# The attention gate's two rows: two f32r products each in place of one f32 product, with the row's two parts in places that rotary rows held at first

## The chip, the cores and the metric

One Trainium2 chip, one core. A time is the device time of one launch in microseconds (us), the median of several runs. Lines of the kernel are named L1088 and so on; engines are TensorE (PE; PEld is its weight load), VectorE (DVE), ScalarE (ACT), GpSimd (POOL) and SyncE (SP), which issues the DMAs.

## The reference

One decoder block on 1024 tokens of 1024 columns, all in float32. The part that matters here is the modulation: one vector `c` gives six rows of 1024 numbers, and the third, `gt_a`, is the gate that scales what the attention half adds to the stream.

```python
cond = jax.nn.silu(c)
mod = (cond @ w_ada[l] + b_ada[l]).astype(x.dtype)
sh_a, sc_a, gt_a, sh_m, sc_m, gt_m = [m[:, None, :] for m in jnp.split(mod, N_MOD, axis=-1)]
h = rms_norm(x, g_attn_pre[l]) * (1 + sc_a) + sh_a
proj = h @ w_in[l]
...
y = mixed @ w_out[l]
x = x + gt_a * rms_norm(y, g_attn_post[l])
h = rms_norm(x, g_mlp_pre[l]) * (1 + sc_m) + sh_m
y = jnp.square(jax.nn.relu(h @ w_up[l])) @ w_down[l]
x = x + gt_m * rms_norm(y, g_mlp_post[l])
```

Between `proj` and `mixed` stand rotary embedding, sliding-window attention with sinks (heads A) and a mixture of three dilated windows (heads B).

## The kernel before

**Number formats.** A product of two f32 tiles takes PE two passes. Where it matters the kernel splits an f32 tile in two parts of the shorter format f32r (a cast gives the high part, a subtraction of it from the original the low part) and multiplies the parts: three products high x high, high x low and low x high where both sides are split (the projection, L920, L921, L923), two where one side is exact in f32r. The subtraction for weights is L555, for probabilities L1326, and the casts are L550 and L1322.

**Stages.** Up to about 113 us the first tokens are normalised, turned round and projected. From there to about 560 us the projection of the rest (`pj`) and the attention run side by side; then come the output projection, and from about 640 us the MLP.

**The order of the work.** The program is written down by a planner in Python (`Sched`). Every step has an engine, a planned duration, the steps that it depends on, the places (`Res`: counted resources, one for each ring of buffers) that it takes and gives back, and a priority. The planner keeps a clock for each engine and always gives out the step that can start first by these clocks. PE's steps lie in streams (projection, scores, transposes, products with values, and so on), each in its own order; the planner picks among their heads. A step of VectorE or GpSimd may have both as its alternatives (the subtraction at L555 has), and the planner gives it to the one that would end first. So a planned duration that changes, or a place given back at another time, changes the order of all engines behind it, and on which of two engines a step runs. On the chip each engine runs its own instructions strictly in that order and waits on semaphores; SyncE's DMAs too are issued in order, and a DMA that has to wait for its buffer holds up those behind it.

**A slice of projection weights.** A load into `w_st` (L541, 128x512, two places), a cast on ScalarE into `w_hl` (L550), a subtraction on VectorE or GpSimd (L555) that frees the `w_st` place. Then the slice serves four groups of three products.

**A pair of attention.** Scores `s_ps` on PE (L1258 for A, L1203 for B), their maximum on VectorE, the exponential on ScalarE (L1278, with the running sum read out), transposes `pt_ps` on PE (L1315 or L1308 and L1311), the split of the transposed tile into `ph` (high part ScalarE L1322, low part VectorE L1326), and the products with the values `o_ps` (L1350, L1338, L1341, L1343), read out by a copy on ScalarE (L1385) and stored (L1395).

**The modulation rows, `ada_piece`.** Three of the rows, which the front does not need at once, are made in 24 pieces between the attention's items: six groups `g` of 512 columns with four pieces each; groups 0 and 1 are the attention gate `gt_a`, 2 to 5 the shift and scale of the MLP. (Groups 6 and 7, the gate of the MLP, go the same way later, during the MLP.) Each piece loads 512 KB of `w_ada` into `wa_st` (L1054) and adds its products with `cond` into `ada_acc` on GpSimd (L1065, L1069, L1070; there is one place for `ada_acc`, `r_adacc`). What is left is a sum over the 128 partitions. For gate rows a product with a tile of ones (step `fin`) sums them and leaves the row in every partition at once. For groups 6 and 7 the accumulator is cast on ScalarE (L1098) and subtracted on VectorE (L1101) into the parts `acc_hl`, and two f32r products with `ones_h` follow (L1086); for groups 0 and 1 one f32 product takes `ada_acc` as it is (L1088), and gives `r_adacc` back. Then come two loads of 256 KB into `gate_st` (the bias, L1112, and the gain, L1113), an addition (L1118) and a multiplication (L1124) on VectorE, and a store to `gate_d` (L1128).

**The places.** `stage(...)` gives one of five places of 4 KB a partition (`r_stg`), shared by `wa_st`, `gate_st`, the split activations `hl` and others. The pool `early` has three more such places: two hold the rotary tables' rows (`turned` L722, `rows` L749) near the start, and all three serve the output projection's first tiles at the end of the attention.

Of the kernel before, what the change touches and what calls it, by code (L numbers as in the profile page):

```python
# [10 lines left out]
F32 = mybir.dt.float32  # L11
F32R = mybir.dt.float32r
# [7 lines left out]
P = 128  # L20
# [157 lines left out]
class Sched:  # L178
# [21 lines left out]
    def op(self, eng, dur, emit, deps=(), **kw):  # L200

        o = self.step(dur, emit, deps, **kw)
        o.alts = None
        if isinstance(eng, str):
            self.queue[eng].append(o)
        else:
            o.alts = dict(zip(eng, zip(dur, emit)))
            for e in eng:
                self.queue[e].append(o)
        return o.ev  # L210

    def pe_op(self, stream, dur, emit, deps=(), **kw):
        o = self.step(dur, emit, deps, **kw)
        o.alts = None
        self.pe.setdefault(stream, []).append(o)
        return o.ev
# [116 lines left out]
def t_as(n):  # L333
    return 0.2 + 0.00083 * n


def t_dv(n):
    return 0.066 + 0.00104 * n
# [19 lines left out]
def hybrid_block(ctx: ExitStack, tc: tile.TileContext, x, positions, w_ada, b_ada, g_attn_post, w_in, w_out,  # L358
# [3 lines left out]
    V, A, G, T = nc.vector, nc.scalar, nc.gpsimd, nc.tensor  # L362
# [3 lines left out]
    op, pe_op = sc.op, sc.pe_op  # L366

    def pool(name, bufs=1, side="left", space=None, stack=ctx):
        kw = dict(name=name, bufs=bufs, reuse_waits="tile")
        if space is not None:  # L370
            kw["space"] = space
        else:
            kw["side"] = side
        return stack.enter_context(tc.tile_pool(**kw))
# [9 lines left out]
    def ring_r(name):  # L384

        return ph2.right.tile([P, 1024], F32, name=name, tag="right")
# [7 lines left out]
    r_stg, r_w, r_wst, r_hl = Res(5), Res(WR), Res(WS), Res(0)  # L394
    r_u, r_raw, r_h2, r_wo = Res(0), Res(0), Res(0), Res(0)
# [11 lines left out]
    ones = const.tile([P, P], F32, name="ones")  # L407
# [21 lines left out]
    early = pool("early", 3)  # L429
# [25 lines left out]
    def stage(name):  # L455
        if st.stgp is None:
            return ring_r(name)
        return st.stgp.tile([P, 1024], F32, name=name, tag="stg")

    def load(emit, nbytes, deps=(), takes=(), prio=5, gives=(), after=None, n=1):  # L460
        return op("SP", nbytes / (345e3 if prio > -500 else 370e3), emit, deps, takes=takes, prio=prio, gives=gives, after=after, n=n)
# [30 lines left out]
    r_wa, r_acc = Res(NWA), Res(2)  # L492
# [90 lines left out]
    e = op("ACT", 0.1, lambda: A.activation(cond[:], c_raw, AF.Exp, scale=-1.0), [e_c], prio=0)  # L583
# [32 lines left out]
    e = op("DVE", 4.2, f_turns, [e_pos, e_c], prio=1)  # L616

    def f_sin():
# [5 lines left out]
                prio=1)  # L624
# [150 lines left out]
    def tables_b():  # L775
# [12 lines left out]
       prio=8)  # L788
# [254 lines left out]
    ada = Tok()  # L1043
    ada.i, ada.acc, ada.e, ada.raw, ada.gate = 0, None, Ev(0.0), {}, {}
    e_mod = {}
    r_adacc = Res(1)

    def ada_piece(i, eng, accp, psum, r_ps, r_acc=None):
        g, jp = divmod(i, 4)
        col = 2 * D + g * 512  # L1050

        def f_load():
            ada.raw[i] = stage("wa_st")
            nc.sync.dma_start(ada.raw[i][:].rearrange("p (j n) -> p j n", j=2),  # L1054
                              ada_view[:, 2 * jp:2 * jp + 2, col:col + 512])
        el = load(f_load, 524288, takes=[(r_stg, 1)], prio=20)

        def f_acc():
            wa = ada.raw.pop(i)[:].rearrange("p (j n) -> p j n", j=2)
            if jp == 0:  # L1060
                ada.acc = accp()
            for j in range(2):
                cj = cond[:, 2 * jp + j:2 * jp + j + 1]
                if jp == 0 and j == 0:
                    eng.tensor_scalar(ada.acc[:, :512], wa[:, 0], cj, 1.0, ALU.mult, ALU.mult)  # L1065
                elif eng is V:
                    V.scalar_tensor_tensor(ada.acc[:, :512], wa[:, j], cj, ada.acc[:, :512], ALU.mult, ALU.add)
                else:
                    G.tensor_scalar(wa[:, j], wa[:, j], cj, 1.0, ALU.mult, ALU.mult)  # L1069
                    G.tensor_tensor(ada.acc[:, :512], ada.acc[:, :512], wa[:, j], ALU.add)  # L1070
        e = op("DVE" if eng is V else "POOL", 1.2 if eng is V else 4.1, f_acc,
               [el, ada.e], takes=[(r_acc or r_adacc, 1)] if jp == 0 else [], gives=[(r_stg, 1)], prio=9)
        ada.e = e
        if jp < 3:
            return
        b = []
        row = g in (0, 1, 6, 7)
        n0 = (g % 2) * 512

        hl = []  # L1080

        def f_fin():
            b.append(psum())
            if row and g > 5:
                for i in range(2):
                    T.matmul(b[0][:, :512], ones_h[:], hl[0][:, i], start=(i == 0), stop=(i == 1))  # L1086
            elif row:
                T.matmul(b[0][:, :512], ones[:], ada.acc[:, :512], start=True, stop=True)  # L1088
            else:
                for k in range(4):  # L1090
                    T.matmul(b[0][:, k:k + 1], ada.acc[:, k * P:(k + 1) * P], ones[:, 0:1], start=True, stop=True)
        if row and g > 5:
            acc = []

            def f_ah():
                acc.append(ada.acc)
                hl.append(stage("acc_hl")[:].rearrange("p (s n) -> p s n", s=2).bitcast(F32R))
                A.copy(hl[0][:, 0], acc[0][:, :512])  # L1098

            def f_al(eng):  # L1100
                return lambda: eng.tensor_tensor(hl[0][:, 1], acc[0][:, :512], hl[0][:, 0].bitcast(F32), ALU.subtract)  # L1101
            e = op("ACT", t_as(512), f_ah, [e], takes=[(r_stg, 1)], prio=4)
            ada.e = e
            e = op("DVE", t_dv(512), f_al(V), [e], gives=[(r_acc or r_adacc, 1)], prio=4)
        ef = pe_op("fin", (0.46 if g > 5 else 0.86) if row else 0.45, f_fin, [e], takes=[(r_ps, 1)],
                   gives=[(r_stg if row and g > 5 else r_acc or r_adacc, 1)])
        if row:
            gate, gp = (gate_d[0], g_attn_post) if g < 2 else (gate_d[1], g_mlp_post)

            def f_gl():  # L1110
                ada.gate[g] = t = stage("gate_st")
                nc.sync.dma_start(t[:, 0:512], b_ada[0:1, col:col + 512].to_broadcast([P, 512]))  # L1112
                nc.sync.dma_start(t[:, 512:1024], gp[0:1, n0:n0 + 512].to_broadcast([P, 512]))  # L1113
            eg = load(f_gl, 524288, [e], takes=[(r_stg, 1)], prio=19)

            def f_g1():
                t = ada.gate[g]
                V.tensor_tensor(t[:, 0:512], b[0][:, :512], t[:, 0:512], ALU.add)  # L1118
            e1 = op("DVE", t_dv(512), f_g1, [ef, eg], gives=[(r_ps, 1)], prio=4)

            def f_g2():
                t = ada.gate[g]
                if g < 2:
                    V.tensor_tensor(t[:, 0:512], t[:, 0:512], t[:, 512:1024], ALU.mult)  # L1124
                else:
                    V.scalar_tensor_tensor(t[:, 0:512], t[:, 0:512], D ** 0.5, t[:, 512:1024], ALU.mult, ALU.mult)
            e2 = op("DVE", t_dv(512), f_g2, [e1], prio=4)
            e_mod[g] = load(lambda: nc.sync.dma_start(gate[:, n0:n0 + 512], ada.gate[g][:, 0:512]), 262144, [e2],  # L1128
                            gives=[(r_stg, 1)], prio=18)
        else:  # L1130
            k0 = n0 // P

            def f_c():
                if g < 4:
                    V.tensor_tensor(s_m[:, k0:k0 + 4], b[0][:, 0:4], cols[:, 40 + k0:44 + k0], ALU.add)
                else:
                    V.tensor_tensor(g_m[:, k0:k0 + 4], b[0][:, 0:4], b1m[:, k0:k0 + 4], ALU.add)
                    V.tensor_tensor(g_m[:, k0:k0 + 4], g_m[:, k0:k0 + 4], cols[:, 16 + k0:20 + k0], ALU.mult)
            e_mod[g] = op("DVE", 0.15, f_c, [ef], gives=[(r_ps, 1)], prio=4)

    def feed_ada():
        if st.d > 1.0 + ada.i * 4.1 / NADA and ada.i < NADA:
            ada_piece(ada.i, G, lambda: adp.tile([P, 512], F32, name="ada_acc", tag="ada_acc", bufs=1), lambda: px.tile([P, 512], F32, name="ada_ps", tag="x"), r_x)
            ada.i += 1
        return ada.i == NADA
# [1097 lines left out]
```

## Time and profile before

| what | us |
|---|---|
| median of 3 runs (lowest, highest) | 1121.01 (1121.01, 1121.78) |
| the profiled execution's own time | 1121.31 |
| its span, first to last instruction | 1119.5 |
| PE busy, 0 to 60 us | 56.00 of 60 |
| PE busy, 60 to 113 us | 51.20 of 53 |
| PE busy, 113 to 235 us | 120.28 of 122 |
| PE busy, 235 to 550 us | 313.65 of 315 |
| PE busy, 550 to 1080 us | 530.00 of 530 |
| PE busy, 1080 us to the end | 31.00 of 39.5 |

The table cuts the span into stretches and asks for the busy time of PE in each. Matmuls are pipelined, so a product that started just before a wait still counts as busy for a while. The granted TensorE clock was 0.998 of full speed over the whole execution. The two `fin` steps of groups 0 and 1 lie at 113.8 and 173.4 us; everything that the change touches is between them and some 60 us behind.

### The profile page before, as it was taken

To read this page: it belongs to the slowest core of one execution; us is meant where nothing else is said; L and a number is where in the kernel's file an instruction comes from. 1 tells how busy PE (TensorE), PEld (TensorE's weight loads), DVE (VectorE), ACT (ScalarE), POOL (GpSimd) and SP (SyncE) were. 2 spreads that over 40 slices of the span, in tenths; PEclk is the share of its full clock that TensorE was granted. 3 is DMA by queue.
4 is the path that set the end of the run, shared out by engine and by line. 5 is a ranking of instruction groups with operands and counts; after the bars stand their busy time and mean duration, and the time that the engine had idled before them with its cause. 6 is when DMAs were issued, how large, how long until landed. Compare 5 with 4: busy or idle time off the path is not lost.

```text
span 1119.5 us, 15561 instructions
## 1 busy us (share of the span) xinstructions
PE 1102.1 (98%) x5393; PEld 917.0 (82%) x5393; DVE 822.5 (73%) x1391; ACT 629.2 (56%) x1092; POOL 245.0 (22%) x313
## 2 busy tenths in 40 slices
PE   8999999999999999999999999999999999999996
PEld 7778787888888888888888888888888888888885
DVE  7868777666677676689798564798643996537998
ACT  8759776464665666576674335653154632247542
POOL 2158758657741231110000000000000000000003
PEclk9999999999999999999999999999999999999999
DMA  9766675554514643656761279521578113584104
GB/s 351 219 197 183 189 226 198 177 178 160 204 33 151 238 136 97 220 226 234 279 244 38 82 239 335 200 62 52 198 262 304 36 57 111 190 316 154 39 19 150
DMA packets 94110, 195.39 MB, mean 175 GB/s; under 512 B 9008, under 2 KB 31664, under 8 KB 94032
## 3 DMA queue, kind: packets, MB, share of 16 engines
q1 hardware_dynamic: 94032, 194.40, 50.4%
q8 instruction: 43, 0.70, 0.2%
q14 instruction: 35, 0.29, 0.1%
HBM read 141.80 MB, written 33.03 MB: 156 GB/s over the span
## 4 chain that ended last, share of the span: by engine, by line
PE 84%; DVE 9%; issue 2%; ACT 2%; DMA 2%; POOL 0%; SPq 0%; DVEq 0%; POOLq 0%; ACTq 0%
PE mlp_ps L2056 17%; PE mlp_ps L2055 17%; PE mlp_ps L2057 17%; PE pj L920 4%; PE pj L923 4%; PE pj L921 4%; PE s_ps L1203 3%; PE y_ps L1609 2%; PE y_ps L1611 2%; PE y_ps L1610 2%; PE o_ps L1338 2%; PE pt_ps L1308 1%; PE o_ps L1350 1%; PE pt_ps L1311 1%; DVE hw L1819 1%
## 5 line engine op out<-in xcount | busy, mean ns | idle before, releaser
L2055 PE MATMUL mlp_ps<-hw 128*128 128x512 f32 x896 | 348.9, 389 | 0.2 <-DVE u L2092 0.2
L2057 PE MATMUL mlp_ps<-hw 128*128 128x512 f32 x896 | 348.6, 389 | 0.0
L2056 PE MATMUL mlp_ps<-hw 128*128 128x512 f32 x896 | 348.6, 389 | 0.0
L2055 PEld LDWEIGHTS mlp_ps<-hw 128*128 128x128 f32 x896 | 168.2, 188 | 35.8 <-DVE u L2092 0.6
L2057 PEld LDWEIGHTS mlp_ps<-hw 128*128 128x128 f32 x896 | 168.2, 188 | 35.0
L2056 PEld LDWEIGHTS mlp_ps<-hw 128*128 128x128 f32 x896 | 168.2, 188 | 34.6
L1819 DVE TENSOR_TENSOR hw<-w,hw 128x1024 fp32r<-128x1024 f32 x96 | 114.5, 1219 | 96.3 <-ACT hw L1812 96.1
L1812 ACT CAST hw<-w 128x1024 fp32r<-128x1024 f32 x96 | 97.7, 1048 | 126.9 <-PE mlp_ps L2057 86.2
L2165 POOL TENSOR_TENSOR st<-st,nhalf 128x1 f32<-128x1 f32 x8 | 8.0, 1011 | 591.8 <-DVE st L2163 591.8
L920 PE MATMUL pj<-hw,w_hl 128*128 128x512 f32 x240 | 101.7, 424 | 0.0
L923 PE MATMUL pj<-hw,w_hl 128*128 128x512 f32 x240 | 94.7, 394 | 0.0
L921 PE MATMUL pj<-hw,w_hl 128*128 128x512 f32 x240 | 94.4, 393 | 0.0
L1326 DVE TENSOR_TENSOR ph<-pt_ps,ph 128x512 fp32r<-128x512 f32 (+1 forms) x110 | 68.8, 646 | 29.3 <-ACT ph L1322 29.0
L1812 ACT CAST hw<-u 128x1024 fp32r<-128x1024 f32 x48 | 48.6, 1051 | 63.2 <-PE mlp_ps L2057 63.2
L1322 ACT CAST ph<-pt_ps 128x512 fp32r<-128x512 f32 (+1 forms) x110 | 58.1, 555 | 28.2 <-PE pt_ps L1311 24.5
L1819 DVE TENSOR_TENSOR hw<-u,hw 128x1024 fp32r<-128x1024 f32 x48 | 56.9, 1217 | 17.8 <-ACT hw L1812 17.8
L1229 ACT ACTIVATE p_sb<-p_sb,mn 128x128 f32<-128x128 f32 (+3 forms) x64 | 49.7, 776 | 32.2 <-DVE mn L1222 31.7
L1234 POOL TENSOR_SCALAR p_sb<-p_sb,den 128x128 f32<-128x128 f32 (+3 forms) x64 | 49.4, 778 | 77.3 <-DVE den L1232 65.2
L2113 DVE TENSOR_TENSOR yacc<-yacc,mlp_ps 128x512 f32<-128x512 f32 x96 | 62.0, 680 | 3.3 <-PE mlp_ps L2057 3.3
L1070 POOL TENSOR_TENSOR ada_acc<-ada_acc,wa_st 128x512 f32<-128x512 f32 x42 | 55.0, 1310 | 3.5
L923 PEld LDWEIGHTS pj<-hw,w_hl 128*128 128x128 f32 x240 | 45.1, 188 | 10.5
L1609 PE MATMUL y_ps<-hw,oh 128*128 128x512 f32 x128 | 52.0, 407 | 0.0
(215 smaller groups left out, 1972.6 us busy)
## 6 DMA issues: line engine op xcount, KB each, us to landing
hw<-s_dram SPq DMA_DIRECT2D x84, 512.0 KB, 4.3
wa_st<-in_w_ada SPq DMA_DIRECT2D x32, 512.0 KB, 4.7
w<-in_w_up SPq DMA_DIRECT2D x32, 512.0 KB, 5.5
w<-in_w_down SPq DMA_DIRECT2D x32, 512.0 KB, 6.9
s_dram<-hw SPq DMA_DIRECT2D x28, 512.0 KB, 3.8
qt<-hl SPq DMA_DIRECT2D x40, 256.0 KB, 2.7
w_st<-in_w_in SPq DMA_DIRECT2D x36, 256.0 KB, 2.8
x_sb<-in_x SPq DMA_DIRECT2D x16, 512.0 KB, 5.5
```

What stands on the lines that cost most here:

```text
L920: T.matmul(ps, w[:, 0, n], h[0], start=(k == 0), stop=False)
L921: T.matmul(ps, w[:, 1, n], h[0], start=False, stop=False)
L923: T.matmul(ps, w[:, 0, n], h[1], start=False, stop=(k == KC - 1))
L1322: A.copy(b["ph"][:, 0, :w], b["pt"][:, :w])
L1326: V.tensor_tensor(b["ph"][:, 1, :w], b["pt"][:, :w], b["ph"][:, 0, :w].bitcast(F32), ALU.subtract)
L1609: T.matmul(ps[:], b["oh"][:, k], wh[:, c0:c0 + 512], start=(k == 4 * m), stop=False)
L1812: A.copy(out[j][0], flat(src[j]))
L1819: V.tensor_tensor(out[j][1], flat(src[j]), out[j][0].bitcast(F32), ALU.subtract)
L2055: T.matmul(ps[m][:], sh, mh, start=starts and k == 0, stop=False, **kw)
L2056: T.matmul(ps[m][:], sh, ml_, start=False, stop=False, **kw)
L2057: T.matmul(ps[m][:], sl, mh, start=False, stop=k == 3, **kw)
L2113: e = op("DVE", t_dv(512), lambda: V.tensor_tensor(y(), y(), ps[m][:], ALU.add), [e, ml.e_y[tb, n]], gives=gives, prio=1)
```

## The change

Groups 0 and 1 now go as groups 6 and 7 do. Their accumulator is cast on ScalarE and subtracted on VectorE into `acc_hl`, and two f32r products with `ones_h` replace the f32 product. Their `acc_hl` lies not in a `stage` place but in the pool `early`; no resource counts that place, since only the rotary rows had it before. `r_adacc` is given back by the subtraction on VectorE and no longer by the product. The planned duration of `fin` goes from 0.86 to 0.46 us for these groups; the cast and the subtraction have planned durations of their own. The next piece's accumulation has the cast as its predecessor (`ada.e = e`) and waits for `r_adacc`.

```diff
@@ -1081,29 +1081,28 @@
 
         def f_fin():
             b.append(psum())
-            if row and g > 5:
+            if row:
                 for i in range(2):
                     T.matmul(b[0][:, :512], ones_h[:], hl[0][:, i], start=(i == 0), stop=(i == 1))
-            elif row:
-                T.matmul(b[0][:, :512], ones[:], ada.acc[:, :512], start=True, stop=True)
             else:
                 for k in range(4):
                     T.matmul(b[0][:, k:k + 1], ada.acc[:, k * P:(k + 1) * P], ones[:, 0:1], start=True, stop=True)
-        if row and g > 5:
+        if row:
             acc = []
 
             def f_ah():
                 acc.append(ada.acc)
-                hl.append(stage("acc_hl")[:].rearrange("p (s n) -> p s n", s=2).bitcast(F32R))
+                t = stage("acc_hl") if g > 5 else early.tile([P, 1024], F32, name="acc_hl", tag="early")
+                hl.append(t[:].rearrange("p (s n) -> p s n", s=2).bitcast(F32R))
                 A.copy(hl[0][:, 0], acc[0][:, :512])
 
             def f_al(eng):
                 return lambda: eng.tensor_tensor(hl[0][:, 1], acc[0][:, :512], hl[0][:, 0].bitcast(F32), ALU.subtract)
-            e = op("ACT", t_as(512), f_ah, [e], takes=[(r_stg, 1)], prio=4)
+            e = op("ACT", t_as(512), f_ah, [e], takes=[(r_stg, 1)] if g > 5 else [], prio=4)
             ada.e = e
             e = op("DVE", t_dv(512), f_al(V), [e], gives=[(r_acc or r_adacc, 1)], prio=4)
-        ef = pe_op("fin", (0.46 if g > 5 else 0.86) if row else 0.45, f_fin, [e], takes=[(r_ps, 1)],
-                   gives=[(r_stg if row and g > 5 else r_acc or r_adacc, 1)])
+        ef = pe_op("fin", 0.46 if row else 0.45, f_fin, [e], takes=[(r_ps, 1)],
+                   gives=[(r_stg if g > 5 else r_wo, int(g > 5))] if row else [(r_acc or r_adacc, 1)])
         if row:
             gate, gp = (gate_d[0], g_attn_post) if g < 2 else (gate_d[1], g_mlp_post)
```

The planner's order is the same on every engine up to about 113 us and again from about 235 us; in between it differs on all of them. Because the diff takes out one line, a line behind it has a number smaller by one in the changed kernel.

PE, first place: the products between the last transposes (`pt_ps`) of one attention pair and the products with values (`o_ps`) that wait for their split, near 127 us. Before, from the second group of transposes on:

```order
L1315 MATMUL pt_ps_1678<-head_65,p_sb_1312 128x128 x4
L920 MATMUL pj_1604<-hw_137,w_hl_1025 128x512
L921 MATMUL pj_1604<-hw_137,w_hl_1025 128x512
L923 MATMUL pj_1604<-hw_137,w_hl_1025 128x512
L1350 MATMUL o_ps_1691<-ph_1676,v_hl_956 128x512 x2
```

Now; the second group of transposes (`pt_ps_1682`) and one product stand just ahead of these rows:

```order
L921 MATMUL pj_1606<-hw_137,w_hl_1025 128x512
L923 MATMUL pj_1606<-hw_137,w_hl_1025 128x512
L920 MATMUL pj_1606<-hw_137,w_hl_1025 128x512
L921 MATMUL pj_1606<-hw_137,w_hl_1025 128x512
L923 MATMUL pj_1606<-hw_137,w_hl_1025 128x512
L920 MATMUL pj_1606<-hw_137,w_hl_1025 128x512
L921 MATMUL pj_1606<-hw_137,w_hl_1025 128x512
L923 MATMUL pj_1606<-hw_137,w_hl_1025 128x512
L920 MATMUL pj_1709<-hw_137,w_hl_1408 128x512
L921 MATMUL pj_1709<-hw_137,w_hl_1408 128x512
L923 MATMUL pj_1709<-hw_137,w_hl_1408 128x512
L1349 MATMUL o_ps_1722<-ph_1675,v_hl_956 128x512 x2
```

In both, three products stand between the first and the second group of transposes. Before, three more stood between the second group and `o_ps`; now it is twelve, one of them ahead of the rows shown. Both pairs of `o_ps` then follow at once, where three products stood between them.

ScalarE, the same place: the casts of weight slices (`w_hl`, L550) and of probabilities (`ph`). Before:

```order
L834 ACTIVATE hl_1616<-pj_1446 128x512
L1278 ACTIVATE p_sb_1533,den4_1536<-p_sb_1533,mn4_1535 128x257 x4
L550 CAST w_hl_1650<-w_st_1522 128x512
L550 CAST w_hl_1665<-w_st_1593 128x512
L1322 CAST ph_1676<-pt_ps_1659 128x512
L1322 CAST ph_1688<-pt_ps_1678 128x512
L1385 COPY otmp_1716<-o_ps_1691 64x512
```

Now:

```order
L550 CAST w_hl_1652<-w_st_1522 128x512
L550 CAST w_hl_1665<-w_st_1573 128x512
L1321 CAST ph_1675<-pt_ps_1660 128x512
L1321 CAST ph_1692<-pt_ps_1682 128x512
L1287 ACTIVATE p_sb_1536<-p_sb_1536,den4_1539 128x256
L834 ACTIVATE hl_1716<-pj_1606 64x512
L550 CAST w_hl_1726<-w_st_1673 128x512
L1277 ACTIVATE p_sb_1718,den4_1721<-p_sb_1718,mn4_1720 128x257
L1384 COPY otmp_1742<-o_ps_1722 64x512
L1321 CAST ph_1750<-pt_ps_1736 128x512
L1321 CAST ph_1758<-pt_ps_1744 128x512
```

The two casts of weights still stand ahead of the two casts of `ph`; the next slice (`w_st_1673`) now stands ahead of the next pair of `ph`, where before (`w_st_1737`) it stood behind it.

SyncE: the loads of weight slices (`w_st`), of the gate's bias and gain (`gate_st`) and of `w_ada` (`wa_st`). Before:

```order
L863 DMA qt_1537<-hl_1454 16x4x512 x2
L1112 DMA gate_st_1566<-in_b_ada 128x512
L1113 DMA gate_st_1566<-in_g_attn_post 128x512
L1395 DMA o_dram3_114<-ot_1569 64x2x128 x2
L541 DMA w_st_1593<-in_w_in 128x512
L1054 DMA wa_st_1621<-in_w_ada 128x2x512
L863 DMA qt_1537<-hl_1616 32x4x512 x2
L783 DMA tab0_150<-rot_dram_177 32x512 x2
L783 DMA tab1_151<-rot_dram_177 32x512 x2
L783 DMA tab0_150<-rot_dram_177 32x512 x2
L783 DMA tab1_151<-rot_dram_177 32x512 x2
L541 DMA w_st_1737<-in_w_in 128x512
```

Now:

```order
L863 DMA qt_1540<-hl_1454 16x4x512 x2
L541 DMA w_st_1573<-in_w_in 128x512
L1394 DMA o_dram3_114<-ot_1581 64x2x128 x2
L1111 DMA gate_st_1610<-in_b_ada 128x512
L1112 DMA gate_st_1610<-in_g_attn_post 128x512
L863 DMA qt_1540<-hl_1614 32x4x512
L1054 DMA wa_st_1630<-in_w_ada 128x2x512
L863 DMA qt_1540<-hl_1614 32x4x512
L541 DMA w_st_1673<-in_w_in 128x512
```

The slice that followed the two gate loads and a store (`w_st_1593`) is now the one ahead of them (`w_st_1573`); the slice after it (`w_st_1673`) moved ahead of the table loads.

On PE the product of group 0, which was the row ahead of the products with `ph_1501`, now stands behind those with `ph_1519`, some fifteen rows on. On VectorE the subtraction of the weight slice ahead of `ph_2332` (L555, at 178 us before) is no longer there; behind it in the plan a slice's subtraction, `w_hl_2237`, stands behind the second gate's addition and multiplication and ahead of `ph_2287` and `ph_2296`. GpSimd makes seven more of the subtractions at L555 between 113 and 235 us, and VectorE that many fewer.

## The prediction

> **What bounds the kernel now.** I read the page first, for the engine that is never idle and for the chain of work that ended last:
>
> ```profile
> PE 1102.1 (98%) x5393; PEld 917.0 (82%) x5393; DVE 822.5 (73%) x1391; ACT 629.2 (56%) x1092; POOL 245.0 (22%) x313
> PE 84%; DVE 9%; issue 2%; ACT 2%; DMA 2%; POOL 0%; SPq 0%; DVEq 0%; POOLq 0%; ACTq 0%
> ```
>
> TensorE (PE) works through 98% of the span and is 84% of the chain. A product less on PE is time less, unless PE then waits for what it would have waited for anyway. So I cut the span where the order of the changed program leaves that of the old one and where it joins it again:
>
> ```profile
> core 0: us, PE busy (x) PEld busy (x) DVE busy (x) ACT busy (x) POOL busy (x), PEclk, DMA share, GB/s
> 113.00:235.00 122.00, 120.28 (x658) 99.72 (x657) 89.65 (x229) 76.50 (x185) 83.41 (x105) 1.00 0.60 190
> ```
>
> The columns are stretch, length, then busy time of each engine. Before 113 us and after about 235 us the two programs have the same instructions in the same order on every engine. In the 122 us between, PE is idle for 1.72 us, at full clock (1.00). What the change does, it does here, and the rest of the program is carried along: with one order on all engines, a PE that is early at 235 us is as early at the end. The idle rows of PE in that stretch are these, with total, times and longest:
>
> ```profile
> PE o_ps L1350 <- DVE ph L1326: 0.8, 2, 0.6
> PE o_ps L1350 <- ACT ph L1322: 0.5, 1, 0.5
> PE o_ps L1338 <- DVE ph L1326: 0.2, 1, 0.2
> ```
>
> All three are the same wait: the product of probabilities and values (o_ps) waits for the split of the transposed probabilities (ph), whose first part ScalarE casts and whose rest VectorE subtracts.
>
> **The products (a gain that is certain).** The chain of waits, cut round each place, gives the time of one gate row on PE:
>
> ```profile
> 112.82 0.44 PE pt_ps L1315 x4
> ...
> 113.97 0.86 PE ada_ps L1088 x2
> 114.82 0.46 PE o_ps L1350 x2
> ...
> 119.01 0.47 PE s_ps L1258 x4
> ...
> 173.53 0.86 PE ada_ps L1088 x2
> ...
> 658.46 0.46 PE ada_ps L1086 x2
> ```
>
> The columns are start, duration, work. An f32 row is one instruction that the profile shows as two passes, 0.86 us together; the MLP gate's rows, which already go in two f32r products, take 0.46 us. Nothing waits in front of either. Two rows: 2 x (0.86 - 0.46) = 0.80 us less on PE. Bounds: 0.80, whatever happens round it, as the chain has no gap beside them.
>
> **What the change adds.** Two casts on ScalarE and two subtractions on VectorE, of a shape that the MLP gate shows:
>
> ```profile
> L1098 ACT CAST acc_hl<-ada_acc x2: 622/622/622, 656.2 to 742.9; 128x512 fp32r<-128x512 f32 x2
> L1101 DVE TENSOR_TENSOR acc_hl<-ada_acc,acc_hl x2: 683/683/683, 657.2 to 743.9; 128x512 fp32r<-128x512 f32 x2
> ```
>
> That is 1.24 us of ScalarE (76.5 busy of 122) and 1.37 us of VectorE (89.65 of 122): both have room, and they cost PE nothing except where a ph is queued behind them. No DMA is added. The places for the two parts are free: the rotary rows left theirs long before.
>
> ```profile
> L772 SPq DMA_DIRECT2D rot_dram<-rows x4: 598/621/703, 77.6 to 79.6; - x4
> ```
>
> **What moves: the first stall.** The larger part lies in the order. PE stood still at 127 us:
>
> ```profile
> 126.88 0.40 PE L923 MATMUL pj<-hw,w_hl 128*128 128x512 f32 x1
> 127.80 0.49 PE L1350 MATMUL o_ps<-ph,v_hl 128*128 128x512 f32 x1 [0.52 <-ACT ph L1322]
> 128.52 0.50 PE L1350 MATMUL o_ps<-ph,v_hl 128*128 128x512 f32 x1 [0.23 <-DVE ph L1326]
> 128.86 0.40 PE L920 MATMUL pj<-hw,w_hl 128*128 128x512 f32 x1
> ```
>
> Products of 512 columns start 0.23 us apart when nothing waits (0.46 for two, above). From 126.88 to 128.86 there are three: 1.98 - 0.69 = 1.29 us lost, more than the bracketed idle time, since the tail of a pipelined product hides the start of a wait. The chain says why:
>
> ```profile
> 120.97 5.59 DMA w_st<-in_w_in
> ...
> 126.64 0.62 ACT w_hl L550
> 127.26 0.49 ACT ph L1322
> ...
> 127.77 0.70 DVE ph L1326
> ```
>
> A slice of weights landed at 126.56; its cast stood at the head of ScalarE's queue, and the cast of ph stood behind it. On SyncE's queue that load was behind two gate loads and a store:
>
> ```profile
> 117.63 1.41 SPq L1112 DMA_DIRECT2D gate_st<-in_b_ada  x1
> ...
> 120.97 0.54 SPq L541 DMA_DIRECT2D w_st<-in_w_in  x1
> ```
>
> In the changed order the load stands ahead of both gate loads, where they stood at 117.63, and its place is freed by GpSimd. It can be issued up to 3.3 us earlier. Independently, PE now has more to do between: from the first group of transposes to the o_ps that waits there were six products and four transposes (6 x 0.23 + 0.44 = 1.82 us), now fifteen and four (3.89 us). So 2.07 us of cover, against 1.29 us lost. Bounds: 0 (the load slips by as much as the cover grows) to -1.29; I take -1.29, as either of two things is enough.
>
> **What moves: the second stall.**
>
> ```profile
> 180.00 0.40 PE L1350 MATMUL o_ps<-ph,v_hl 128*128 128x512 f32 x1
> 181.01 0.50 PE L1350 MATMUL o_ps<-ph,v_hl 128*128 128x512 f32 x1 [0.61 <-DVE ph L1326]
> 181.34 0.40 PE L920 MATMUL pj<-hw,w_hl 128*128 128x512 f32 x1
> ...
> 178.58 1.77 DVE L555 TENSOR_TENSOR w_hl<-w_st,w_hl 128x512 fp32r<-128x512 f32 x1 [0.56 <-ACT w_hl L550]
> ...
> 178.52 1.28 POOL L1070 TENSOR_TENSOR ada_acc<-ada_acc,wa_st 128x512 f32<-128x512 f32 x1
> ```
>
> Two products in 1.34 us instead of 0.46: 0.88 lost. The subtraction of a weight slice took 1.77 us on VectorE, where the gate's subtraction of the same shape took 0.68: it began 0.06 us after GpSimd had begun an addition of 1.28 us, and ran for as long again after it as it takes alone. In the changed order that slice is subtracted on GpSimd and the o_ps have 2.16 us and more of PE work in front of them. Bounds 0 to -0.88; I take -0.88.
>
> The Trainium skill ("SBUF — State Buffer", section "Who interferes with whom") has the rule: a VectorE instruction with two SBUF inputs contends with a GpSimd instruction that reads SBUF, and the one that comes second is blocked for the whole of the first. The trace agrees (1.77 beside 0.68). It speaks against this change, whose two added subtractions read both inputs from SBUF. By the rule they take up to 0.68 + 1.28 us each, and the sum grows by what of that reaches a ph, which is the first rival below.
>
> **What comes new.** (1) The next weight slice. Its cast now stands ahead of two ph casts, as the old one did. Its place is freed by a subtraction on VectorE near 125.6 us (the cast before it began at 124.25 and took 0.61; the subtraction takes about as long again). The loads of 110 to 125 us:
>
> ```profile
> w_st<-in_w_in SPq DMA_DIRECT2D x2, 256.0 KB, 4.3
> ...
> wa_st<-in_w_ada SPq DMA_DIRECT2D x1, 512.0 KB, 6.5
> ...
> gate_st<-in_g_attn_post SPq DMA_DIRECT2D x1, 256.0 KB, 6.4
> ```
>
> The last column is us from issue to landing. And the rows of ScalarE and SyncE round the place, where the old program loaded and read:
>
> ```profile
> 123.76 0.50 ACT L1278 ACTIVATE p_sb<-p_sb,mn 128x257 f32<-128x257 f32 x1
> ...
> 124.25 0.61 ACT L550 CAST w_hl<-w_st 128x512 fp32r<-128x512 f32 x1
> ...
> 127.16 1.07 ACT L1322 CAST ph<-pt_ps 128x512 fp32r<-128x512 f32 x2
> ...
> 130.03 0.37 SPq L541 DMA_DIRECT2D w_st<-in_w_in  x1
> 130.28 0.58 ACT L1385 COPY otmp<-o_ps 64x512 f32<-64x512 f32 x1 [2.04 <-PE o_ps L1350]
> ```
>
> Landed at 129.9 (4.3) to 132.1 (6.5), then the cast (0.61), an exponential (0.50), a copy (0.58) and the ph cast (0.54, half of 1.07): ph is ready at 132.2 to 134.4, its rest 0.7 later, and needed 0.23 later. PE reaches that o_ps after 61 products of 512 columns, 24 of 256 and 16 transposes (0.23, 0.117, 0.11 each: 18.6 us) from 113.97, so at 132.5. Bounds 0.2 to 2.3; I take 0.7, nearer the low end, because the load of this stretch is one gate pair and one wa_st, and both are issued 3 us or more ahead. (2) Before another pair of ph the second gate's product and a weight slice's subtraction now stand on VectorE, with 1.94 us of PE work (four transposes 0.44, five products of 512 columns 1.15, two of 384 0.35) to cover the subtraction and the ph, as against 1.82 at either stall above. Bounds 0 to 0.88 (what such a subtraction cost at 181 us); I take 0.2, near the low end, since a subtraction of 0.68 instead of 1.77 would have cost nothing even there.
>
> **Sum.** The profiled execution took 1121.31 us (span 1119.5 and 1.8 around it), 0.30 above the median of the runs, 1121.01. 1121.31 - 0.80 - 1.29 - 0.88 + 0.7 + 0.2 = 1119.24; on the median's footing **1118.9 us**, 0.19% less.
>
> **Rivals.**
> *A, given back through VectorE.* The two new subtractions and the weight slice ahead of ph each meet an addition on GpSimd, which is busy for 83 of the 122 us. For: 1.77 above. Against: the new subtractions have a cast of ScalarE running beside them, and where ph follows, PE has over 3 us of work in front. Price 0.6 + 0.88 + 0.7: the relief of 2.17 is gone and 0.80 is left: 1120.2.
> *B, slower: the head of a queue waits for a load.* The stall of 127 us comes back at place (1), longer, and then at (2), where VectorE waits for a gate load that now stands later in its queue. For: 6.5 us is shown. Against: the slice is issued near 125.6, earlier than the 130.03 of the slice that held its turn. It decides from 2.97 us of new stalls; with a freeing subtraction held up by 1.1 us, a landing of 6.5 and 2.0 at the gate it is 3.4 + 2.0 = 5.4: 1121.0 - 2.97 + 5.4 = 1123.4.
> *C, all waits close.* The remaining idle time (1.72 - 0.52 - 0.23 - 0.61 = 0.36, with three hidden tails of 0.16 about 0.9) goes too and nothing new comes: -0.80 - 2.17 - 0.9: 1117.1.
> *D, the change doesn't do what it says:* a cast waits for the rotary rows' place. The row of 79.6 us speaks against it; then the time is the old one, 1121.0.
>
> **How the numbers follow.** A measurement of this kernel tells 0.2% (2.24 us) from no change: faster is under 1118.8, slower over 1123.3. Forecast 0.50 (its own range 1118.0 to 1119.8, half of it below 1118.8), A 0.16, C 0.19, B 0.13, D 0.02. Faster: 0.25 + 0.19 = 0.44; slower 0.13; same 0.25 + 0.16 + 0.02 = 0.43. The range runs from just past C (1116.9) past A and D to where four fifths of B's new stalls stand: 1121.0 - 2.97 + 0.8 x 5.4 = 1122.4.
>
> **What would show it.** In the changed profile: the two rows at L1086 with 0.46 on the chain and no wait in front; no idle time of over 0.2 us for o_ps near 127 us; no subtraction at L555 on VectorE that PE waits for near 180 us; at 235 us PE about 2 us earlier, and from there all to the end shifted by that. Wrong if PE waits at o_ps after the third weight cast for over 1 us, if VectorE waits for gate_st with ph behind, or if PE at 235 us is not earlier than by 0.8.

## The result, and the profile after

| | median us | lowest to highest | runs |
|---|---|---|---|
| before | 1121.68 | 1120.26 to 1123.04 | 14 |
| changed | 1123.92 | 1121.50 to 1124.68 | 14 |

The changed kernel is slower: the ratio of the times is 1.0017, with a 95% interval of 1.0009 to 1.0024. (When it was timed again, below as after_again, the ratio was 1.0004, and its interval holds no change.) The profiled execution took 1123.13 us (span 1121.4). The page's busy line and its shares of the chain:

```profile
PE 1101.7 (98%) x5393; PEld 916.7 (82%) x5393; DVE 820.0 (73%) x1388; ACT 629.6 (56%) x1092; POOL 252.3 (22%) x320
PE 80%; DVE 9%; ACT 4%; DMA 3%; issue 3%; POOL 1%; SPq 1%; POOLq 0%; DVEq 0%; ACTq 0%
```

PE is busy 0.4 us less and holds less of the chain (80% for 84%); DMA and ScalarE hold more. Asked for the waits of PE from 113 to 240 us (for what, total, times, longest), the trace gives:

```profile
PE o_ps L1349 <- ACT ph L1321: 1.7, 1, 1.7
PE pv L891 <- DVE ot L1373: 1.4, 1, 1.4
PE o_ps L1349 <- DVE ph L1325: 0.2, 1, 0.2
```

The 1.72 us that PE stood idle before have become 3.3, in two places. PE's rows show what went as forecast and what didn't (timeline of PE, three places):

```profile
118.80 0.63 PE L1257 MATMUL s_ps<-kt,qt 128*128 128x256 f32 x4
119.28 0.63 PE L1086 MATMUL ada_ps<-acc_hl,ones_h 128*128 128x512 f32 x2
119.75 0.39 PE L920 MATMUL pj<-hw,w_hl 128*128 128x512 f32 x1
...
129.25 0.40 PE L923 MATMUL pj<-hw,w_hl 128*128 128x512 f32 x1
129.49 0.87 PE L1349 MATMUL o_ps<-ph,v_hl 128*128 128x512 f32 x3
...
133.14 0.39 PE L923 MATMUL pj<-hw,w_hl 128*128 128x512 f32 x1
135.19 0.50 PE L1349 MATMUL o_ps<-ph,v_hl 128*128 128x512 f32 x1 [1.66 <-ACT ph L1321]
135.92 0.50 PE L1349 MATMUL o_ps<-ph,v_hl 128*128 128x512 f32 x1 [0.23 <-DVE ph L1325]
```

The gate row takes 119.75 - 119.28 = 0.47 us, with no wait. The o_ps of the old first stall starts at 129.49, straight behind its product. The next o_ps should start at 133.37 and starts at 135.19: with the second step, 0.73 instead of 0.23, that is 1.82 + 0.50 = 2.3 us lost. The chain of waits shows behind what, and the same for the second place:

```profile
125.00 0.78 DVE w_hl L555
...
125.80 6.98 DMA w_st<-in_w_in
...
132.80 0.02 ACT w_hl L550
...
133.32 0.60 ACT p_sb L1277 x2
...
133.94 0.59 ACT otmp L1384
...
188.16 3.19 DMA o_dram<-ot
...
191.47 0.43 DVE ot L1373
...
191.94 0.66 PE pv L891 x4
```

First place: the load of a weight slice, issued when the subtraction of 125.00 had freed its place, took 6.98 us to land. Its cast stood at the head of ScalarE's queue, and behind it an exponential, a copy and the two casts of ph. Second place, not in the forecast: a store of the attention's output had to land before VectorE had a place to write the next output (`ot`, two places). That write reads PSUM, and PE's `pv` waited until it had ended. `pv` would have started at 190.42 (0.11 us behind the transpose ahead of it) and started at 191.94: 1.5 us.

To compare runs, one stretch of PE is used: from the last transposes ahead of the first gate row (112.66 us before, 113.48 after) to a projection product behind the last difference of the orders (224.08 and 225.71). It took 111.42 us before and 112.22 in this execution of the changed kernel. The rest of the difference of the two profiled executions (1.82) lies ahead of the stretch (0.82) and behind it (0.2), where the orders are the same.

### The profile page after: what moved, and what is told of

It reads as the page before. It is cut to its first block, busy times and chain, and to the rows that moved or that the text cites. A ratio compares the mean times of both kernels' runs of the same rounds, so it can differ in the third digit from the quotient of the medians.

```text
span 1121.4 us, 15565 instructions
## 1 busy us (share of the span) xinstructions
PE 1101.7 (98%) x5393; PEld 916.7 (82%) x5393; DVE 820.0 (73%) x1388; ACT 629.6 (56%) x1092; POOL 252.3 (22%) x320
## 4 chain that ended last, share of the span: by engine, by line
PE 80%; DVE 9%; ACT 4%; DMA 3%; issue 3%; POOL 1%; SPq 1%; POOLq 0%; DVEq 0%; ACTq 0%
PE mlp_ps L2056 17%; PE mlp_ps L2054 17%; PE mlp_ps L2055 16%; PE pj L920 4%; PE pj L923 3%; PE pj L921 3%; PE s_ps L1202 3%; PE y_ps L1608 2%; PE y_ps L1610 2%; PE y_ps L1609 2%; PE o_ps L1337 2%; PE pt_ps L1307 1%; PE pt_ps L1310 1%; ACT p_sb L1277 1%; DVE hw L1818 1%
## 5 line engine op out<-in xcount | busy, mean ns | idle before, releaser
L1233 POOL TENSOR_SCALAR p_sb<-p_sb,den 128x128 f32<-128x128 f32 (+3 forms) x64 | 49.1, 774 | 78.1 <-DVE den L1231 68.5
```

## The experiments

All times are medians of 6 to 12 executions, with the kernel before timed beside them (30 to 33 executions). The ratio is an estimate of its own and not the quotient of the two medians. "Profiled" is the time of the one execution whose trace is read; "stretch" and "idle" are from that trace, so they belong to this time and not to the median. "Idle" is PE's in the stretch by the trace's waits, at o_ps near 135 us and at pv near 192 us.

| run | us | before beside it | ratio, 95% interval | profiled | stretch | idle at o_ps | at pv |
|---|---|---|---|---|---|---|---|
| prod_only | 1120.44 | 1121.26 | 1.0000, 0.9991 to 1.0009 | 1121.68 | 110.62 | - | - |
| order_only | 1121.81 | 1121.26 | 1.0009, 0.9996 to 1.0021 | 1124.58 | 114.65 | 2.4 | 2.6 |
| third_w_st | 1119.01 | 1121.26 | 0.9982, 0.9972 to 0.9992 | 1121.31 | 112.82 | 2.4 | 0 |
| third_ot | 1119.50 | 1121.26 | 0.9991, 0.9982 to 1.0000 | 1119.50 | 110.04 | 0.7 | 0 |
| after_again | 1122.27 | 1121.74 | 1.0004, 0.9994 to 1.0013 | 1123.71 | 114.23 | 2.1 | 3.0 |
| late_cast | 1121.09 | 1121.74 | 1.0001, 0.9991 to 1.0011 | 1119.39 | 109.68 | 0 | 1.3 |
| late_cast_ot | 1118.58 | 1121.74 | 0.9970, 0.9959 to 0.9981 | 1117.27 | 108.27 | 0 | 0 |
| before_ot | 1121.75 | 1121.74 | 0.9999, 0.9989 to 1.0009 | 1120.97 | 110.90 | - | - |
| fixed_again | 1118.39 | 1121.28 | 0.9971, 0.9961 to 0.9981 | 1117.45 | 108.26 | 0 | 0 |
| fixed_f32 | 1118.78 | 1121.28 | 0.9979, 0.9970 to 0.9988 | 1119.77 | 108.85 | 0 | 0 |
| wa_late | 1120.53 | 1121.28 | 0.9996, 0.9987 to 1.0005 | 1122.12 | 112.72 | 0 | 2.8 |
| stage_hl | 1120.36 | 1121.28 | 0.9996, 0.9987 to 1.0005 | 1119.98 | 109.78 | 0.7 | 0 |

The profiled execution is not always a middling one: those of order_only and third_w_st are the slowest of their runs, those of late_cast and late_cast_ot the fastest.

### Is it the products or the order?

prod_only puts the new products into the old order. Against the changed kernel, for the attention gate's groups alone, and with the product planned at 0.86 us as before:

```diff
+                if todo and g < 2:
+                    todo.pop()()
...
-            e = op("ACT", t_as(512), f_ah, [e], takes=[(r_stg, 1)] if g > 5 else [], prio=4)
-            ada.e = e
-            e = op("DVE", t_dv(512), f_al(V), [e], gives=[(r_acc or r_adacc, 1)], prio=4)
...
+            else:
+                todo.append(f_al(V))
+                op("DVE", 0.0, lambda: todo and todo.pop()(), [op("ACT", 0.0, f_ah, [e], prio=4)], prio=4)
```

> The order of the kernel before on every engine, with the two f32r products, the casts and the subtractions put in where they fit (the planner sees them as free and keeps 0.86 us for the product). Theory (the new order's two waits cost the time, the products are a gain): before minus 0.8, 1120.9 us on a median of 1121.7; from the last transposes ahead of the first row (112.66 us) to 221.6 us PE takes 108.2 us instead of 108.97; the stall of 1.29 us at 127 us and that of 0.88 us at 181 us are still there. Rival 1 (the gain of a shorter row is swallowed by the next wait, whose end a load or another engine sets): 1121.7, no change. Rival 2 (the added casts and subtractions hold up a split of the probabilities): 1122.5 or more, with a new wait for ph.

The stretch fell by 0.80 us (111.42 to 110.62), but not in the expected way. The two products of the first row waited in line:

```profile
PE ada_ps L1088 <- DVE acc_hl L1102: 0.6, 1, 0.6
PE ada_ps L1088 <- ACT acc_hl L1099: 0.3, 1, 0.3
```

In exchange o_ps lost 0.3 us at 128 us, where it had lost 1.29, and nothing at 181 us: a PE that comes later finds ph ready. So the 0.80 of this stretch is a balance of several terms, and not yet a proof that the shorter rows count. The interval of the time (0.9991 to 1.0009) doesn't tell 0.8 us from nothing.

order_only is the other half: the changed order with the old product.

```diff
-            if row:
+            if row and g < 2:
+                T.matmul(b[0][:, :512], ones[:], acc[0][:, :512], start=True, stop=True)
+            elif row:
...
```

> The changed order on every engine, but the f32 product of before in place of cast, subtraction and two f32r products for the attention gate's rows (a second place for the accumulator keeps it free of a race). Theory (order's waits): the waits at 135 us (2.4 us) and at 192 us (1.6 us) stay, and the time is that of the changed kernel, 1123.9, plus 0.8 less what those waits swallow of it, so 1123.9 to 1124.7. Rival (casts, subtractions or f32r products are what costs): back to the 1121.7 of before.

Both waits are there with no cast, subtraction or f32r product of the gate in the program:

```profile
PE pv L891 <- DVE ot L1377: 2.6, 1, 2.6
PE o_ps L1353 <- ACT ph L1325: 2.2, 1, 2.2
```

So the waits are the order's. The time, 1121.81, is some 2 us less than expected (0.55 above before), and its interval holds no change too; the trace with the two waits is that of the slowest execution, 1124.58.

### The wait at 192 us: a place for ot

third_ot gives the tile a third real place. The planner goes on counting two, so no instruction moves:

```diff
-        opool = pool("op", NO, **kw)
+        opool = pool("op", NO + 1, **kw)
```

> The changed kernel, same order on every engine, with a third real place for the attention's output tile ot (the planner still counts two), so that VectorE at 188.7 us no longer waits until 191.35 for a store to land. Theory: the stall of 1.58 us at 192 us is gone and the time is 1122.3. Rival (the next wait, a ph or a load, takes its place at once): 1123.9, with an idle PE within some us behind.

The wait is gone and none took its place at once. The time, 1119.50, is lower than expected, against the 1123.92 of the other comparison (the changed kernel was not timed in this one); the wait at o_ps was also shorter in this trace (the load landed 5.78 us after its issue). before_ot is the same edit to the kernel before:

> The kernel before with a third real place for ot, same order. Theory (only the new order waits for a store of ot): no change from before, within 0.5 us. Rival (a third place helps in any order, and what third_ot won is no matter of the change): 1 us or more below before.

No change, as expected (ratio 0.9999): what the place wins, it wins in the new order alone.

### The wait at 135 us: what the load waits for

> The changed kernel, same order on every engine, with a third real place for weight slices (the planner still counts two), so that the load issued at 125.80 us no longer waits for the subtraction that ended at 125.78 and can follow the load at 123.82. Theory: it is issued at 124.4 and lands 1.4 us earlier, the stall of 2.4 us at 135 us falls to about 1.0, and the time is 1122.5. Rival (the load lands when the queued traffic is through, whenever it was issued): stall unchanged, 1123.9.

```diff
-            t = w_raw[u, i] = prp.tile([P, 512], F32, name="w_st", tag="w_st", bufs=WS)
+            t = w_raw[u, i] = prp.tile([P, 512], F32, name="w_st", tag="w_st", bufs=WS + 1)
```

In the execution that was profiled the rival was right about this wait. Timeline of third_w_st:

```profile
122.11 1.47 SPq L541 DMA_DIRECT2D w_st<-in_w_in  x1
...
130.97 0.62 ACT L550 CAST w_hl<-w_st 128x512 fp32r<-128x512 f32 x1 [3.73 <-DMA w_st<-in_w_in]
```

Counted from the start of the stretch (111.10 in this trace), the load was issued at 11.0 instead of 12.3, and its cast began at 19.9 instead of 19.3: no sooner. The other traces say the same: in all ten of the changed order, this one included, in which the load of `w_ada` stands ahead of the slice, the slice landed 1.9 to 2.2 us after that load, though it was issued 1.4 to 2.9 us after it.

The wait for ot was absent in this trace. SyncE's rows show when its stores went out. In the changed kernel:

```profile
177.45 0.33 SPq L541 DMA_DIRECT2D w_st<-in_w_in  x1
...
179.82 0.54 SPq L541 DMA_DIRECT2D w_st<-in_w_in  x1
...
185.62 0.68 DVE L1389 TENSOR_TENSOR ot<-o_ps,otmp 64x512 f32<-64x512 f32 x1 [0.95 <-ACT otmp L1384]
185.68 0.59 SPq L863 DMA_DIRECT2D kt<-hl  x1
...
186.37 0.54 SPq L541 DMA_DIRECT2D w_st<-in_w_in  x1
...
186.95 0.45 SPq L1054 DMA_DIRECT2D wa_st<-in_w_ada  x1
...
187.50 1.28 SPq L1394 DMA_DIRECT2D o_dram<-ot  x2
```

The output was ready at 186.30 and its stores were issued at 187.50 and 188.16: SyncE still had two loads to issue ahead of them, at some 0.6 us each. It had issued one DMA straight behind the other since 177.45, when a slice's load went out that had waited 3.1 us for its place. So some 1.2 of the 1.5 us at pv can be put down to SyncE's queue. The landing varies too: the second store landed 3.2 us after its issue here, and 4.4 to 4.9 in order_only, after_again and wa_late, whose waits at pv are the longest. In third_w_st the stores were issued when the output was ready:

```profile
177.51 0.53 SPq L541 DMA_DIRECT2D w_st<-in_w_in  x1
...
185.43 0.68 DVE L1389 TENSOR_TENSOR ot<-o_ps,otmp 64x512 f32<-64x512 f32 x1 [0.95 <-ACT otmp L1384]
186.14 1.28 SPq L1394 DMA_DIRECT2D o_dram<-ot  x2
```

But SyncE was not ahead. The row of 177.51 is the one that stands at 179.82 above; counted from the start of each stretch they are at 66.4 and 66.3 us, and the second store landed at 78.1 us here and at 77.9 in the changed kernel. What differs is PE: it had lost 2.2 us more at the first wait and behind it, and reached the row ahead of `pv` at 79.0 us instead of 76.8, when the store had landed. The first loss hid the second wait, and the stretch, 112.82 us, is no shorter than the 112.22 of the changed kernel. So this trace does not show why the median of third_w_st is 2.3 us below that of before. The execution gained its 1.8 us on the changed kernel's profiled one ahead of the stretch, which began at 111.10 instead of 113.48. The cause stays open.

wa_late tests whether the traffic ahead of the slice makes it late. The load of `w_ada` that stood ahead of it is issued behind it:

```diff
+            while late:
+                late.pop()()
...
-            ada.raw[i] = stage("wa_st")
-            nc.sync.dma_start(ada.raw[i][:].rearrange("p (j n) -> p j n", j=2),
-                              ada_view[:, 2 * jp:2 * jp + 2, col:col + 512])
+            def go():
+                ...
+            late.append(go) if i == 5 else go()
```

> The changed kernel with one load moved: the 512 KB of w_ada that are issued at 123.08 us come behind the 256 KB of the weight slice issued at 125.80 us. Theory (the slice lands when the loads ahead of it are through, so third_w_st's earlier issue gained nothing): with 512 KB less ahead of it, at some 350 GB/s, it lands 1.5 us sooner after its issue, 5.5 us instead of 7.0, and the wait at 135 us is 1 to 1.5 us shorter. Rival (a load of that kind takes 7 us there, whatever is ahead): landing 6.5 us or more after issue, wait unchanged.

```profile
123.80 0.33 SPq L542 DMA_DIRECT2D w_st<-in_w_in  x1
...
127.58 0.61 ACT L553 CAST w_hl<-w_st 128x512 fp32r<-128x512 f32 x1
```

The slice landed at 127.08, 3.3 us after its issue, where it had taken 7.0 (5.8 to 7.6 over the nine traces in which it is issued behind the load of `w_ada` and has two places) and 5.5 was expected. The wait at o_ps is gone. The stretch is no shorter for it: PE came to `pv` 2.5 us earlier than in the changed kernel's trace, waited there for 2.8 us, and then ran at a lower clock for some 3 us (last section). The Trainium skill ("DMA: Bandwidth & Descriptors", section "Queues, rings and completion order") says that SyncE's DMAs share one ring on each DMA engine and that descriptors are taken in ring order. The trace agrees: with 512 KB put behind it the slice landed 3.7 us sooner after its issue, and an issue 1.3 us earlier behind the same loads took off nothing.

### Moving the cast, and both together

late_cast leaves the load alone and moves the one cast that holds the queue:

```diff
+            if len(n_hi) == 18:
+                w_hl[a] = None
+                late.append(hi)
+                return
...
             A.copy(b["ph"][:, 0, :w], b["pt"][:, :w])
+            if late:
+                n_late.append(1)
+                if len(n_late) == 2:
+                    for f in late:
+                        f()
...
```

> The changed kernel with one cast moved: that of the weight slice whose load is issued at 125.80 us stands behind the next two casts of the probabilities on ScalarE instead of ahead of them; every other row keeps its place. Theory (the cast held the probabilities behind a load): the wait at 135 us goes, 1.2 to 3.0 us, and the time falls by about 2 against the changed kernel. Rival (another wait at the same place takes over, the copy of o_ps or VectorE): a wait of 1 us or more stays for the same o_ps.

The wait at o_ps is gone and no other stands there. Beside it the changed kernel was run again:

> The changed kernel once more, so that it stands in one comparison with the three below. Theory: between 1122.5 and 1124, slower than before by 1 to 2.5 us; waits of PE at 135 us (1.2 to 3.0 us in the traces so far) and at 192 us (0 to 2.9 us) again. Rival (the difference to before is drawn by where the loads of the start fall, not by the order): the same time as before.

Its median, 1122.27, is 1.2 us above late_cast's, less than the 2 expected, and the ratios to before (1.0004 and 1.0001) don't tell the two apart. In this comparison the changed kernel can't be told from before either (0.9994 to 1.0013); in its trace the waits were 2.1 and 3.0 us. Times of one kernel lie 2 to 6 us apart, and for the changed kernel the two waits are probably part of that: over seven traces of its order, or nearly its order, with two places for ot, pv waited 0, 0, 1.3, 1.4, 2.6, 2.8 and 3.0 us.

> Late_cast with the third place for ot. Theory (the two waits are the whole loss, and they add): 3 to 4.5 us below the changed kernel, so 2 to 3 us below before, 1118 to 1119; PE takes 108.5 us for the stretch in which before took 111.42 and the changed kernel 112.22. Rival (they don't add: the one wait hides behind the other): no faster than the better of third_ot and late_cast alone.

1118.58, and the stretch 108.27 us, both as expected: the two losses add. The ratio, 0.9970 with an interval up to 0.9981, lies below those of late_cast and, just, of third_ot. Asked for the waits of PE from 112 to 224 us, the trace names none. Its row of the window from 113 to 235 us:

```profile
113.00:235.00 122.00, 122.00 (x679) 102.78 (x678) 88.79 (x232) 78.82 (x191) 92.25 (x115) 1.00 0.64 198
```

PE works through all of the 122 us (120.28 before, 118.75 in the changed kernel).

> Late_cast_ot once more, beside the next one. Theory: 1118.5, 3 us below before; no wait of PE over 0.3 us between 113 and 222 us.

> Late_cast_ot with the f32 product of before for the two rows: ScalarE copies the accumulator in full f32 where it cast it, VectorE subtracts nothing, and one f32 product of the copy takes the place of the two f32r products; the order is the same. Where nothing waits, a row's products must show in full. Theory: 0.80 us above fixed_again (109.07 us of PE for the stretch that took 108.27). Rival (the shorter product is swallowed somewhere): within 0.2 us of fixed_again in that stretch.

fixed_again took 1118.39. Against it fixed_f32 has 0.59 us more in the stretch, where 0.80 was expected, and 0.39 us more in the median, which its interval can't tell from nothing. In these two traces the shorter rows count for three quarters of their 0.80 us where nothing waits behind them.

### The place of the parts

```diff
-                t = stage("acc_hl") if g > 5 else early.tile([P, 1024], F32, name="acc_hl", tag="early")
+                t = stage("acc_hl")
```

> The changed kernel with the parts of the two rows in one of the five shared places, as the MLP gate's are, instead of those that the rotary rows held. The order of TensorE and ScalarE is that of the changed kernel; a few rows of VectorE, GpSimd and SyncE move. Theory (the place of the parts matters little, the order that both share matters): the wait at 135 us stays, over 1 us, and the time is within 1.5 us of the changed kernel's. Rival (the place of the parts decides, since it holds or frees a load): no wait at 135 us, or 2 us of difference.

The wait at o_ps stays, but at 0.7 us, where over 1 was expected (the slice landed 5.8 us after its issue), and the one at pv was absent. The time is 1.9 us below the 1122.27 of after_again, in another comparison; by the ratios to before (0.9996 and 1.0004) the two can't be told apart. Whether the places of the rotary rows cost anything stays open.

## Why the prediction was wrong

Forecast were 1118.9 us and a range of 1116.9 to 1122.4; measured were 1123.92. Of the miss 0.7 us is the footing: the forecast started from 1121.01, the median of three executions, and beside the changed kernel the old one took 1121.68. The rest, and the direction, is in the terms.

- **The products: right in kind.** 0.47 us for a row on PE and no wait in front. The stretch shows 0.59 of the 0.80 us where nothing waits (fixed_f32 against fixed_again). That prod_only shows just 0.80 is luck, since several terms balance there.
- **The two old stalls: right.** Neither is there; -1.29 and -0.88 were both earned. In late_cast_ot, where nothing new waits, the stretch is 3.15 us shorter than before, against the 2.97 that the three gains sum to; the third old wait, 0.2 us, is gone there as well.
- **What comes new, (1): right in place, wrong in size.** This is the step that failed first. It took 0.7 from bounds of 0.2 to 2.3, with a landing between 4.3 and 6.5 us. In a trace that ran 0.82 later, PE's arrival (133.37) came as worked out, and the issue (125.80) 0.6 us earlier; the landing took 6.98, and 2.3 us were lost, the upper bound and 1.6 more than was taken. The reason given for the low end was the error: "the load of this stretch is one gate pair and one wa_st, and both are issued 3 us or more ahead". They were issued about that far ahead (121.28 to 123.08), but that is not enough for them to be through: they are 1 MB, the slice queues behind them, and wa_late shows what half of it costs: 3.7 us of landing time.
- **What comes new, (2): about right.** The second gate's load was in time. The subtraction ahead of that ph took 1.76 us beside a subtraction of `hl` on GpSimd that had begun 0.5 us earlier. PE has no named wait there, but the four products behind it take 1.22 us (177.24 to 178.46) instead of 0.92: 0.3 us for the 0.2 that was taken.

```profile
174.01 1.71 POOL L826 TENSOR_TENSOR hl<-hl 128x512 fp32r<-128x512 f32 x1
...
174.51 1.76 DVE L555 TENSOR_TENSOR w_hl<-w_st,w_hl 128x512 fp32r<-128x512 f32 x1
...
177.24 1.38 PE L1349 MATMUL o_ps<-ph,v_hl 128*128 128x512 f32 x4
```

- **A wait that the sum lacked.** This is the second step that failed: the sum put nothing for it. The store of ot stood behind two loads in SyncE's queue and had to land before the next output could be written, 1.5 us at pv. The prediction looked at the queues ahead of ph alone.
- **The sum, with measured terms:** -0.80 - 1.29 - 0.88 + 2.3 + 1.5 = +0.8, which is what the stretch shows in that execution (112.22 - 111.42), closer than the single terms are known. In after_again the same waits were longer and the stretch 2.8 us over the old one. The medians' 2.24 lie between.
- **The rivals.** B had the kind right, and its first place: the head of a queue waits for a load. Its second place was wrong, and its price, 5.4 us of new waits, is about what the longest trace shows (2.1 and 3.0 us of idle time, with the tails some 6 us). It had 0.13, which was too little. A's contention is in the trace (the 1.76 above) and cost 0.3 us at most; the two added subtractions took 0.66 and 0.68, so they met none of it. (The 1.77 us of the old program ran on for 0.55 us behind the end of the addition, and not for the 0.68 that it takes alone.) In the whole program three subtractions at L555 moved to GpSimd (18 to 21), and not seven as was read from the order; its other four new instructions are two of `hl` and two of `p_sb`. C's condition, that all waits close, holds in late_cast_ot, which gains 3.15 us in the stretch where C had 3.87.

## What to carry to other kernels

A change that shortens one step of a planned program also deals out a new order, and the order may cost more than the step wins: read from the new order, for every queue, which load or store stands at the head of work that PE waits for, and add up the bytes issued just ahead of it. A load's landing time is no property of the load; the same 256 KB took 3.3 to 8.8 us by what was still on its way ahead of it. When two waits follow each other, one can hide the other, so a run that removes the first alone need not gain. When work waits for a place that a store still holds, a real place that the planner doesn't count can remove the wait and moves no instruction, which makes it a clean experiment and, here, half of a version that beats both kernels (1118.4 to 1118.6 us).

## What the hardware showed beside this

After some long waits PE ran on at half its clock. Windows of third_w_st round its wait (stretch, length, busy times, then the granted clock, third from the end):

```profile
130.00:133.00 3.00, 1.13 (x5) 0.58 (x4) 0.27 (x1) 1.98 (x5) 2.92 (x4) 1.00 0.36 87
133.00:135.00 2.00, 1.41 (x4) 0.76 (x5) 2.00 (x4) 2.00 (x7) 1.22 (x1) 1.00 0.82 231
135.00:138.00 3.00, 3.00 (x13) 2.58 (x12) 1.77 (x4) 1.93 (x5) 2.42 (x5) 0.52 0.61 214
138.00:140.00 2.00, 2.00 (x9) 1.65 (x9) 0.69 (x1) 0.59 (x1) 1.92 (x3) 0.86 0.21 55
```

For some 3 us behind a wait of 2.4 us the clock was 0.52. Row for row and counted from the start of the stretch, PE was 0.56 us behind the changed kernel's trace at that o_ps and 2.16 us behind at 142 us: 1.6 us are the clock's. wa_late shows the same behind its 2.8 us (0.60 from 189 to 192 us), but order_only and after_again, with waits of 2.4 to 3.0 us, kept 1.00. The Trainium skill ("TensorE: Matmul & The Clock Gate", "Part 1: The HAM clock gate") gives half rate after an idle window of about 3.4 us that runs free of the program. That the same wait is punished in one execution and not in another fits a free-running window; that 2.4 us were enough is less than the page's figure. Why these two waits and not the others is not shown.

The mean clock of each execution is on record, and the two profiled executions with such a spell have 0.996, the others 0.997 to 0.999. Of the changed kernel 9 of 26 executions had 0.996 (1124.1 us on average, the others 1122.3); of the kernel before 8 of the 94 with a clock on record had it (1123.7, the others 1121.5). So part of the changed kernel's loss may be such spells, more frequent behind its longer waits; no run here takes the two apart.
